# Weaving the xbc projection into the S5 and RG-LRU mixers, and giving the last attention head's norms a step of their own

## The chip, the cores and the metric

One core of one Trainium2 chip runs the whole kernel. The metric is the device time of one execution in microseconds (us), as the median of three runs. The engines are TensorE (PE, with its weight load PEld), VectorE (DVE), ScalarE (ACT), GpSimd (POOL) and SyncE (SP), whose queue issues nearly all transfers.

## The reference

Input x is 1024 frames of 1024 features, in two residual blocks. Block 1 is a modulated layer norm, a retention and gated-linear-attention mixer, an output projection and an MLP. Block 2, in which the change lies, is this:

```
proj = x @ w_in                       # split into z, xbc, dt, s5 input, rg input, rg gate
xbc  = silu(causal_conv4(proj_xbc))   # 1024 features, feeds the SSD mixer
s5   : complex diagonal scan h_n = A h_{n-1} + V u, y = readout(h) + local part, gelu, GLU
rg   : x = causal_conv4(proj_rgx); r, g = gates(x)
       h_n = a_n h_{n-1} + sqrt(1 - a_n^2) * g * x, with a from r;  out = h * gelu(proj_gate)
y    = concat(ssd, s5, rg) @ w_out,  residual and layer norm -> h1
attn : 4 heads of 256, over a given memory (softmax(q K^T) V Wo, summed over heads), residual, layer norm -> h2
mlp  : squared-relu MLP on h2, residual, layer norm
```

## The kernel before

All large products are fp32 by three products of rounded halves: `mm3` (L114 to L116) issues high x high, high x low and low x high, each 128x512. A split into halves is a cast on ACT (L82) and a subtraction on DVE (L83); weights come through a staging page S (L91). Features stand on the partitions, two halves h of 512 frames make the columns, so a projection to 128 features takes 2 x 24 = 48 products, 24 into each of two PSUM buffers.

SBUF pages of 128x1024 come from pools (X 8, H 8, W 8, U 4, S 6, bc 3 buffers). Each engine runs its instructions in order. That order is made by a scheduler from dependences and from the order of the code: earlier code goes first where it is ready by the scheduler's own costs, later code fills in where it is not.

`build` runs, in block 2: `dt_proj`, `s5_mixer`, `xbc_proj`, `rg_mixer`, then the SSD blocks woven with the output projection, attention, MLP. The three in the middle are written one after another.

- `s5_mixer`: input transposes, the V products (L1584), a DVE chain of scans and a complex multiplication (L1591 to L1598, `cmul` L1360 to L1365) that gives H; loads of the kernel matrix K in 16 parts (L1609) and of P in two (L1614); the readout, 16 groups of one product with K (L1625) and two with P and H (L1628) for each half m, 48 in all; an addition on DVE (L1638), transposes (L1644), gelu, GLU (L1661 to L1667).
- `xbc_proj`: eight tiles j of 128 features, weights for two at a time. Per half, ACT copies the product (L1193) and makes the last tap (L1194); DVE adds three taps (L1176); ACT takes tanh (L1197); DVE closes the silu (L1198); SP writes it out (L1199).
- `rg_mixer`: projection and convolution; gate weights Wg; plain fp32 gate products (L1329, L1332) with Sigmoid and Tanh; Ln, Exp, Exp and Sqrt on ACT (L1338 to L1343, with the scan L1345 on DVE); then the products of Wg (two tiles, 96 products) whose results are read at L1351 and L1352.
- `attention`: eight parts (4 heads x 2 halves h) in `pipe`, which at each step advances every live part, the oldest first. A part has three steps: scores and softmax; transposes of the probabilities (L1727) and the V products; the Wo products (L1753), added to the residual `acc`. For the last head, hd == 3, the third step also norms each finished tile (`normalize`, L155 to L171), stores it and transposes it (`to_T`: L182 on PE, L186 and the split L82 and L83) for the MLP, whose results ACT reads at L767.

PSUM tiles are all named ps here; `order` rows give them numbers.

Of the kernel before, what the change touches and what calls it, by code (L numbers as in the profile page):

```python
# [14 lines left out]
S = 1024  # L15
# [1046 lines left out]
class Mix2(Mix1):  # L1062
# [116 lines left out]
    def xbc_proj(self, T):  # L1179
        nc, I = self.nc, self.I  # L1180
        hw = self.small([128, 40], tag="hw", bufs=1)
        nc.vector.tensor_scalar(out=hw[:, 0:32], in0=self.pvec("ssd_conv_w"), scalar1=0.5, scalar2=None, op0=ALU.mult)
        nc.vector.tensor_scalar(out=hw[:, 32:40], in0=self.pvec("ssd_conv_b"), scalar1=0.5, scalar2=None, op0=ALU.mult)
        self.s_xd = self.dram([128, 8, S], "s_xbc")
        for c in range(4):
            W = self.wcols(I["w_in_2"], 512 + 256 * c, 256)
            for m in range(2):
                j = 2 * c + m
                raw, o = self.page("X"), self.page("X")
                for h in range(2):  # L1190
                    sl = slice(512 * h, 512 * h + 512)
                    ps = self.feat_out(T, W, slice(128 * m, 128 * m + 128), h)
                    nc.scalar.copy(out=raw[:, sl], in_=ps)  # L1193
                    nc.scalar.activation(out=o[:, sl], in_=ps, func=ACTF.Identity, scale=hw[:, 4 * j + 3:4 * j + 4],  # L1194
                                         bias=hw[:, 32 + j:33 + j])
                self.conv(o, raw, hw[:, 4 * j:4 * j + 4])
                nc.scalar.activation(out=raw, in_=o, func=ACTF.Tanh)  # L1197
                nc.vector.scalar_tensor_tensor(out=o, in0=raw, scalar=1.0, in1=o, op0=ALU.add, op1=ALU.mult)  # L1198
                nc.sync.dma_start(out=self.s_xd[:, j, :], in_=o)  # L1199

    def ssd_setup(self):
        self.s_St = self.half()
# [88 lines left out]
    def rg_mixer(self, T):  # L1291
# [19 lines left out]
        for m in range(2):  # L1311
            raw, xc = self.page("X"), self.page("X")
            for h in range(2):
                sl = slice(512 * h, 512 * h + 512)
                ps = self.feat_out(T, Wx, slice(128 * m, 128 * m + 128), h)
                nc.scalar.copy(out=raw[:, sl], in_=ps)
                nc.scalar.activation(out=xc[:, sl], in_=ps, func=ACTF.Identity, scale=cw[:, 4 * m + 3:4 * m + 4],
                                     bias=cb[:, m:m + 1])
            self.conv(xc, raw, cw[:, 4 * m:4 * m + 4])
            xcs.append(xc)  # L1320
        Wg = self.wcols(w, 2056, 256)
        ms = []
        for m in range(2):
            xc = xcs[m]
            r, gx, t = self.page("H"), self.page("H"), self.page("H")
            for h in range(2):
                sl = slice(512 * h, 512 * h + 512)
                ps = self.ps("tr")
                nc.tensor.matmul(out=ps, lhsT=gw[:, 0, m], rhs=xc[:, sl], start=True, stop=True)  # L1329
                nc.scalar.activation(out=r[:, sl], in_=ps, func=ACTF.Sigmoid, bias=ba[:, m:m + 1])  # L1330
                ps = self.ps("tr")
                nc.tensor.matmul(out=ps, lhsT=gw[:, 1, m], rhs=xc[:, sl], start=True, stop=True)  # L1332
                nc.scalar.activation(out=gx[:, sl], in_=ps, func=ACTF.Tanh, scale=0.5, bias=sm[:, 6 + m:7 + m])
            nc.scalar.activation(out=t, in_=r, func=ACTF.Tanh, scale=sm[:, 2 + m:3 + m])
            nc.vector.scalar_tensor_tensor(out=gx, in0=gx, scalar=1.0, in1=xc, op0=ALU.add, op1=ALU.mult)
            ms.append((xc, r, gx, t))
        for m, (xc, r, gx, t) in enumerate(ms):
            nc.scalar.activation(out=xc, in_=t, func=ACTF.Ln, bias=1.0)  # L1338
            nc.scalar.activation(out=xc, in_=xc, func=ACTF.Exp, scale=-1.0)
            nc.scalar.activation(out=r, in_=r, func=ACTF.Exp, scale=sm[:, m:m + 1])  # L1340
            nc.vector.tensor_tensor(out=t, in0=t, in1=xc, op=ALU.mult)
        for m, (xc, r, gx, t) in enumerate(ms):
            nc.scalar.activation(out=t, in_=t, func=ACTF.Sqrt, scale=0.5)  # L1343
            nc.vector.tensor_tensor(out=gx, in0=gx, in1=t, op=ALU.mult)
            nc.vector.tensor_tensor_scan(out=t, data0=r, data1=gx, initial=0.0, op0=ALU.mult, op1=ALU.add)  # L1345
        for m, (xc, r, gx, t) in enumerate(ms):
            x, q = self.page("X"), self.page("X")
            for h in range(2):
                sl = slice(512 * h, 512 * h + 512)
                ps = self.feat_out(T, Wg, slice(128 * m, 128 * m + 128), h)  # L1350
                nc.scalar.activation(out=x[:, sl], in_=ps, func=ACTF.Copy, scale=0.5)  # L1351
                nc.scalar.activation(out=q[:, sl], in_=ps, func=ACTF.Square)  # L1352
            self.gelu(x, q, q)
            nc.vector.tensor_tensor(out=t, in0=t, in1=q, op=ALU.mult)
            nc.sync.dma_start(out=self.rg_od[:, m, :], in_=t)
# [192 lines left out]
    def s5_mixer(self, T):  # L1548
# [19 lines left out]
        for m in range(2):  # L1568
            for q in range(2):
                ps = self.ps("tr")  # L1570
                for j in range(4):
                    g = 4 * q + j
# [17 lines left out]
        Are, Aim, t = page(), page(), self.page("H")  # L1590
# [12 lines left out]
        a = [v3(x)[:, :, i0] for x in (Are, Aim)]  # L1603
        p = [v3(x)[:, :, i0] for x in (co, sn)]
        self.cmul(v3(H[0])[:, :, i1], v3(H[1])[:, :, i1], a, p, v3(t)[:, :, i1])
        M = [self.page("H") for _ in range(2)]
        for m in range(2):
            for s in range(8):
# [9 lines left out]
        for m in range(2):  # L1618
            ps = self.ps("sc").rearrange("p (r a c) -> p r a c", r=2, c=128)
            for j in range(4):  # L1620
                a = 4 * m + j
                for r in range(2):
                    rs = slice(64 * r, 64 * r + 64)
                    g = 2 * a + r
# [22 lines left out]
                nc.scalar.activation(out=q[:, sl], in_=ps, func=ACTF.Square)  # L1647
            self.gelu(x, q, x)
            Y.append(x)
        gw = self.half([128, 2, 256])  # L1650
        nc.sync.dma_start(out=gw, in_=I["s5_glu_w_2"].rearrange("(k p) e -> p k e", p=128))
        gb = self.small([128, 8], tag="s5t", bufs=20)
# [2 lines left out]
        for m in range(2):  # L1655
            g, o = self.page("H"), self.page("H")
# [25 lines left out]
    def attn_part(self, T, hd, h, st8):  # L1682
# [55 lines left out]
        for t4 in range(4):  # L1738
            t = 4 * h + t4
# [8 lines left out]
            for n in range(2):  # L1748
# [1 line left out]
                ps = self.ps("sc")[:, 0:512]  # L1750
                self.mm3(ps, [(oh[:, m, ts], ol[:, m, ts]) for m in range(2)], [(a[:, 0, c], b[:, 0, c]) for a, b in Wo])
                self.add_res(acc[t][:, c], ps, hd == 0)
            if hd == 3:  # L1753
                if t == 0:
                    st8["T"] = self.new_T()
                self.normalize(acc[t], acc[t], True)
                nc.sync.dma_start(out=_rows(self.h2d, t), in_=acc[t])
                self.to_T(acc[t], t, st8["T"], self.pvec("ln2_g_2"), self.pvec("ln2_b_2"))
# [24 lines left out]
def build(tc, I, out):  # L1783
    from contextlib import ExitStack
    with ExitStack() as ctx:
        n = Mix2(tc, ctx, I, out)
        n.modulation()
        n.kv_mem()
        def run(g):
            while True:  # L1790
                try:
                    next(g)
                except StopIteration as e:
                    return e.value
# [7 lines left out]
        T, steps = None, [3, 0, 1, 0, 1]  # L1802
        while T is None:
# [4 lines left out]
            T = next(norm)  # L1808
# [11 lines left out]
        T = run(n.block1_out())  # L1820
        T = n.block1_mlp(T)
        n.dt_proj(T)
        n.s5_mixer(T)
        n.xbc_proj(T)
        n.rg_mixer(T)
        n.ssd_setup()
        n.wout = n.wout_load(I["w_out_2"])
        out = n.block2_out()
# [90 lines left out]
```

## Time and profile before

| what | value |
|---|---|
| median of three runs | 2733.69 us (2730.89 to 2739.81) |
| the profiled execution, its own time | 2723.2 us |
| its span | 2721.4 us |
| mean granted TensorE clock | 0.964 |
| PE busy | 2572.5 us (95%) |
| DVE busy | 1908.2 us (70%) |
| ACT busy | 1113.8 us (41%) |

PE is busy nearly throughout, and a busy matmul record says nothing of the clock it ran at: a granted clock of 1.00 is the higher level (2.4 GHz), 0.50 the lower (1.2 GHz). The tables by stretch give both side by side, the timeline gives the distance from one instruction to the next. Some matmul records are missing from the trace, and one plain fp32 product shows as two records.

### The profile page before, as it was taken

How to read it: one execution, taken by the hardware profiler on the slowest of the kernel's cores; microseconds unless marked ns; L12 is line 12 of the kernel's file. 1: busy time of each engine (PE TensorE's matmuls, PEld its weight loads, DVE VectorE, ACT ScalarE, POOL GpSimd, SP SyncE). 2: the span in 40 equal slices, each digit the busy share in tenths (PEclk: the TensorE clock that was granted, in tenths of full speed). 3: DMA queues.
4: the chain of work that ended last, by engine and by line, in shares of the span. 5: the costliest groups of instructions: out<-in, count | busy, mean ns of one | idle time of the engine just before them, and what ended most of it. 6: DMA issues, size and time to landing. Idle time of an engine off the chain costs nothing.

```text
span 2721.4 us, 32892 instructions
## 1 busy us (share of the span) xinstructions
PE 2572.5 (95%) x12086; PEld 2085.6 (77%) x12086; DVE 1908.2 (70%) x3237; ACT 1113.8 (41%) x1669; POOL 265.8 (10%) x238
## 2 busy tenths in 40 slices
PE   7898999889999999999999997999997999999997
PEld 7576777677888888888876765778876888888885
DVE  5847765788897777555954558785566877767759
ACT  3522233224654444433642462452236444444332
POOL 4112135540000000000000004200000000000000
PEclk8899999999999999999997998999998999999998
DMA  9674423454266669857641313371101756699774
GB/s 332 210 232 142 147 98 102 142 150 147 78 224 217 214 234 324 287 177 240 202 153 47 110 62 105 111 242 40 54 21 73 246 195 224 230 325 333 271 234 145
DMA packets 255130, 484.36 MB, mean 178 GB/s; under 512 B 21604, under 2 KB 110964, under 8 KB 254968
## 3 DMA queue, kind: packets, MB, share of 16 engines
q1 hardware_dynamic: 247768, 470.59, 51.3%
q10 hardware_dynamic: 7200, 11.67, 1.2%
q8 instruction: 95, 1.56, 0.2%
q14 instruction: 67, 0.55, 0.1%
HBM read 338.80 MB, written 143.38 MB: 177 GB/s over the span
## 4 chain that ended last, share of the span: by engine, by line
PE 76%; DVE 10%; DMA 4%; ACT 4%; issue 3%; POOL 2%; SPq 0%; ACTq 0%; DVEq 0%; POOLq 0%
PE ps L114 23%; PE ps L116 23%; PE ps L115 23%; ACT half L186 1%; PE ps L182 1%; DMA H<-r_qk 1%; DVE half L543 1%; POOL X L522 1%; DMA H<-g_qkb 1%; DMA bc<-in_w_ada 1%; DVE st L155 1%; PE ps L1628 1%; DVE W L83 1%; PE ps L535 1%; POOL W L83 0%
## 5 line engine op out<-in xcount | busy, mean ns | idle before, releaser
L114 PE MATMUL ps<-U,W 128*128 128x512 f32 (+1 forms) x1080 | 426.2, 395 | 11.4 <-ACT X L1352 5.9
L83 DVE TENSOR_TENSOR W<-S,W 128x1024 fp32r<-128x1024 f32 (+1 forms) x272 | 332.8, 1225 | 147.9 <-ACT W L82 145.9
L114 PE MATMUL ps<-W,H 128*128 128x512 f32 x1088 | 425.1, 391 | 3.6 <-DVE sm L167 3.0
L115 PE MATMUL ps<-U,W 128*128 128x512 f32 (+1 forms) x1080 | 424.1, 393 | 0.1
L115 PE MATMUL ps<-W,H 128*128 128x512 f32 x1088 | 424.0, 390 | 0.0
L116 PE MATMUL ps<-W,H 128*128 128x512 f32 x1088 | 423.9, 390 | 0.0
L116 PE MATMUL ps<-U,W 128*128 128x512 f32 (+1 forms) x1080 | 423.5, 392 | 0.0
L82 ACT CAST W<-S 128x1024 fp32r<-128x1024 f32 x288 | 299.2, 1043 | 282.0 <-PE ps L115 200.0
L83 DVE TENSOR_TENSOR H<-S,H 128x1024 fp32r<-128x1024 f32 x130 | 158.8, 1222 | 149.3 <-ACT H L82 138.5
L82 ACT CAST H<-S 128x1024 fp32r<-128x1024 f32 x130 | 136.5, 1050 | 288.6 <-PE ps L115 211.9
L114 PEld LDWEIGHTS ps<-U,W 128*128 128x128 f32 (+1 forms) x1080 | 201.1, 186 | 59.9 <-ACT X L1352 6.3
L114 PEld LDWEIGHTS ps<-W,H 128*128 128x128 f32 x1088 | 204.6, 188 | 47.7 <-DVE X L1014 3.7
L115 PEld LDWEIGHTS ps<-U,W 128*128 128x128 f32 (+1 forms) x1080 | 201.1, 186 | 47.0 <-DVE U L336 2.5
L116 PEld LDWEIGHTS ps<-W,H 128*128 128x128 f32 x1088 | 204.4, 188 | 42.2 <-DVE H L83 0.2
L115 PEld LDWEIGHTS ps<-W,H 128*128 128x128 f32 x1088 | 204.6, 188 | 41.9
L116 PEld LDWEIGHTS ps<-U,W 128*128 128x128 f32 (+1 forms) x1080 | 200.7, 186 | 45.0 <-issue 0.7
L114 PE MATMUL ps<-W,U 128*128 128x512 f32 x352 | 142.0, 403 | 0.0
L115 PE MATMUL ps<-W,U 128*128 128x512 f32 x352 | 140.6, 399 | 0.2 <-DVE W L83 0.2
L116 PE MATMUL ps<-W,U 128*128 128x512 f32 x352 | 140.4, 399 | 0.1
L767 ACT ACTIVATE ev<-ev 128x512 f32<-128x512 f32 x104 | 65.5, 630 | 138.8 <-DVE ev L865 117.3
L1239 POOL TENSOR_TENSOR half<-tri,s_adt 128x512 f32<-128x512 f32 x16 | 19.6, 1233 | 884.5 <-DVE half L1116 778.2
L768 ACT ACTIVATE X<-ev 128x512 f32<-128x512 f32 x128 | 81.1, 636 | 3.5
(527 smaller groups left out, 4606.5 us busy)
## 6 DMA issues: line engine op xcount, KB each, us to landing
S<-mlp_h SPq DMA_DIRECT2D x112, 512.0 KB, 4.8
S<-in_w_ff SPq DMA_DIRECT2D x96, 512.0 KB, 5.1
mlp_h<-X SPq DMA_DIRECT2D x96, 512.0 KB, 3.9
S<-in_mlp_w SPq DMA_DIRECT2D x96, 512.0 KB, 5.2
mlp_w<-S SPq DMA_DIRECT2D x96, 256.0 KB, 2.8
S<-mlp_w SPq DMA_DIRECT2D x48, 512.0 KB, 4.8
S<-in_w_in SPq DMA_DIRECT2D x46, 512.0 KB, 5.2
bc<-in_w_ada SPq DMA_DIRECT2D x32, 512.0 KB, 5.0
```

Source lines behind the costliest of these rows:

```text
L82: self.nc.scalar.copy(out=hi, in_=src)
L83: (lo_eng or self.nc.vector).tensor_tensor(out=lo, in0=src, in1=hi.bitcast(F32), op=ALU.subtract)
L114: mm(out=ps, lhsT=lh, rhs=rh, start=start and k == 0, stop=False)
L115: mm(out=ps, lhsT=lh, rhs=rl, start=False, stop=False)
L116: mm(out=ps, lhsT=ll, rhs=rh, start=False, stop=stop and k == n - 1)
L155: self.nc.vector.bn_stats(out=st[:, h, :], in_=y[:, h * 512:(h + 1) * 512])
L182: nc.tensor.transpose(ps[:, j * 128:(j + 1) * 128], y[:, k * 128:(k + 1) * 128], self.ident)
L186: nc.scalar.activation(out=full[:, j * 128:(j + 1) * 128], in_=ps[:, j * 128:(j + 1) * 128], func=ACTF.Identity, scale=scale[:, k:k + 1], ...
L522: nc.gpsimd.tensor_tensor(out=E[:, l, :].rearrange("p (g c) -> p g c", c=2 * w), in0=bv, in1=bv[:, :, w - 1:w].broadcast_to([128, 64 // w, ...
L535: nc.tensor.matmul(out=ps[:, r, u, :], lhsT=k[rs] if l < 0 else E[rs, l, :], rhs=q[rs] if l < 0 else qt[rs, l, :], start=True, stop=True)
L767: nc.scalar.activation(out=r, in_=x, func=ACTF.Relu)
L768: nc.scalar.activation(out=out, in_=r, func=ACTF.Square)
```

## The change

`xbc_proj` becomes a generator that yields after each feature tile, and its two pages per tile come from the pools S and bc instead of X. `s5_mixer` yields after H is made and before the GLU; `rg_mixer` yields after the convolutions, after the gates and after the scans. `build` advances the xbc generator at those points: three tiles after s5's first yield and one after its second, one after rg's first and three after its second. In attention the norms, the store and the transposes of the last head leave the Wo loop and become a fourth step of their part, so that `pipe` runs those of h = 0 beside the third step of h = 1.

```diff
@@ xbc_proj
-                raw, o = self.page("X"), self.page("X")
+                raw, o = self.page("S"), self.page("bc")
...
                 nc.sync.dma_start(out=self.s_xd[:, j, :], in_=o)
+                yield
@@ rg_mixer
             xcs.append(xc)
+        yield
         Wg = self.wcols(w, 2056, 256)
...
             ms.append((xc, r, gx, t))
+        yield
         for m, (xc, r, gx, t) in enumerate(ms):
             nc.scalar.activation(out=xc, in_=t, func=ACTF.Ln, bias=1.0)
...
             nc.vector.tensor_tensor_scan(out=t, data0=r, data1=gx, initial=0.0, op0=ALU.mult, op1=ALU.add)
+        yield
         for m, (xc, r, gx, t) in enumerate(ms):
             x, q = self.page("X"), self.page("X")
@@ s5_mixer
         self.cmul(v3(H[0])[:, :, i1], v3(H[1])[:, :, i1], a, p, v3(t)[:, :, i1])
+        yield
         M = [self.page("H") for _ in range(2)]
...
             Y.append(x)
+        yield
         gw = self.half([128, 2, 256])
@@ attn_part
-            if hd == 3:
-                if t == 0:
-                    st8["T"] = self.new_T()
+        if hd == 3:
+            yield
+            if h == 0:
+                st8["T"] = self.new_T()
+            for t in range(4 * h, 4 * h + 4):
                 self.normalize(acc[t], acc[t], True)
                 nc.sync.dma_start(out=_rows(self.h2d, t), in_=acc[t])
                 self.to_T(acc[t], t, st8["T"], self.pvec("ln2_g_2"), self.pvec("ln2_b_2"))
@@ build
-        n.s5_mixer(T)
-        n.xbc_proj(T)
-        n.rg_mixer(T)
+        xbc = n.xbc_proj(T)
+        for g, side in ((n.s5_mixer(T), (3, 1)), (n.rg_mixer(T), (1, 3))):
+            for _ in g:
+                for _ in range(side[0] if side else 0):
+                    next(xbc, None)
+                side = side[1:]
+        run(xbc)
```

Lines behind an inserted yield shift: the readout's L1625 and L1628 become L1630 and L1633, `cmul` L1360 to L1365 become L1364 to L1369, the scans L1598 become L1602, the transposes L1727 become L1733.

On PE, at the readout of s5, this is where xbc's first tile (its second PSUM buffer is ps1984) ends before:

```order
L116 MATMUL ps1984_11966<-U956_6101,W1980_11933 128x512
L1625 MATMUL ps1952_11792<-H1947_11768,X1929_11677 128x128
L1625 MATMUL ps1958_11841<-H1948_11769,X1930_11678 128x128
L1628 MATMUL ps1952_11792<-H1949_11786,X1945_11758 128x128
L1628 MATMUL ps1958_11841<-H1949_11786,X1945_11758 128x128
```

And the same place now; ps1961 belongs to xbc's second tile, ps1970 to its third, ps1977 to the readout:

```order
L116 MATMUL ps1961_11875<-U956_6101,W1953_11780 128x512
L114 MATMUL ps1970_11922<-U954_6099,W1963_11909 128x512
L115 MATMUL ps1970_11922<-U955_6100,W1963_11909 128x512
L1630 MATMUL ps1977_12006<-H1972_11982,X1929_11677 128x128
L116 MATMUL ps1970_11922<-U954_6099,W1964_11910 128x512
```

Before, the whole readout stands behind 48 products of xbc and the other seven tiles behind the readout. Now tiles 0, 1 and 2 and a part of tile 3 stand ahead of the first product with P (L1633, 62 rows further down), and 46 products of the readout stand together inside tile 3.

On DVE, at the end of s5's scans and in its complex multiplication, before:

```order
L1361 TENSOR_TENSOR X1945_11758<-X1942_11747,H1939_11741 128x8x127
L1598 SCALAR_TENSOR_TENSOR X1943_11748<-H1941_11743,X1943_11748 128x1024
L1364 TENSOR_TENSOR X1946_11759<-X1942_11747,H1940_11742 128x8x127
L1360 TENSOR_TENSOR H1944_11749<-X1943_11748,H1940_11742 128x8x127
L1362 TENSOR_TENSOR X1945_11758<-X1945_11758,H1944_11749 128x8x127
L1363 TENSOR_TENSOR H1944_11749<-X1943_11748,H1939_11741 128x8x127
L1365 TENSOR_TENSOR X1946_11759<-X1946_11759,H1944_11749 128x8x127
```

Now, with bc1955 the first tile of xbc, and W1964 the low half of the weights of its third and fourth:

```order
L1368 TENSOR_TENSOR X1946_11759<-X1942_11747,H1940_11742 128x8x127
L1364 TENSOR_TENSOR H1944_11749<-X1943_11748,H1940_11742 128x8x127
L1176 SCALAR_TENSOR_TENSOR bc1955_11785<-S1954_11784,hw1947_11768,bc1955_11785 128x1023
L1366 TENSOR_TENSOR X1945_11758<-X1945_11758,H1944_11749 128x8x127
L1176 SCALAR_TENSOR_TENSOR bc1955_11785<-S1954_11784,hw1947_11768,bc1955_11785 128x1022
L1367 TENSOR_TENSOR H1944_11749<-X1943_11748,H1939_11741 128x8x127
L1176 SCALAR_TENSOR_TENSOR bc1955_11785<-S1954_11784,hw1947_11768,bc1955_11785 128x1021
L1369 TENSOR_TENSOR X1946_11759<-X1946_11759,H1944_11749 128x8x127
L1198 SCALAR_TENSOR_TENSOR bc1955_11785<-S1954_11784,bc1955_11785 128x1024
L83 TENSOR_TENSOR W1964_11910<-S1962_11908,W1963_11909 128x1024
```

The three taps of xbc's first tile stand inside the multiplication that gives H, and the split of the next weights behind the tile's last step. In SP's queue the writes (L1199) of the first two xbc tiles now stand ahead of the two loads of P; before, the loads of P stood ahead of every such write.

On PE, at the end of attention, before; ps2600 to ps2635 are transposes of normed tiles of h = 0, ps2642 is a V product of h = 1:

```order
L182 MATMUL ps2600_15884<-ident_75,X2386_14547 128x128 x4
L182 MATMUL ps2602_15896<-ident_75,X2386_14547 128x128 x4
L1727 MATMUL ps2637_16082<-ident_75,half2584_15819 128x128 x4
L1727 MATMUL ps2637_16082<-ident_75,half2587_15839 128x128 x4
L182 MATMUL ps2611_15942<-ident_75,X2389_14569 128x128 x4
L182 MATMUL ps2613_15954<-ident_75,X2389_14569 128x128 x4
L182 MATMUL ps2622_16000<-ident_75,X2392_14591 128x128 x4
L182 MATMUL ps2624_16012<-ident_75,X2392_14591 128x128 x4
L182 MATMUL ps2633_16058<-ident_75,X2395_14613 128x128 x4
L182 MATMUL ps2635_16070<-ident_75,X2395_14613 128x128 x4
L114 MATMUL ps2642_16097<-H2638_16091,bc2546_15541 128x512
```

Now, behind all 12 V products of h = 1; ps2644 and ps2645 are its first Wo products, ps2613 to ps2622 transposes of h = 0:

```order
L114 MATMUL ps2645_16123<-W2567_15706,H2600_15923 128x512
L182 MATMUL ps2613_15965<-ident_75,X2386_14547 128x128 x4
L116 MATMUL ps2644_16115<-W2567_15706,H2601_15924 128x512
L115 MATMUL ps2645_16123<-W2568_15707,H2600_15923 128x512
L114 MATMUL ps2644_16115<-W2570_15712,H2600_15923 128x512
L115 MATMUL ps2644_16115<-W2571_15713,H2600_15923 128x512
L116 MATMUL ps2645_16123<-W2567_15706,H2601_15924 128x512
L114 MATMUL ps2645_16123<-W2570_15712,H2600_15923 128x512
L182 MATMUL ps2615_15977<-ident_75,X2386_14547 128x128 x4
L182 MATMUL ps2622_16007<-ident_75,X2389_14569 128x128 x4
```

Before, the V and Wo products of h = 1 stand behind every transpose of h = 0; now the V products stand ahead of them and the Wo products between them. On ACT the cast of the probabilities of h = 1 stands ahead of the first norm of h = 0 instead of behind the last one but a tile's rest.

## Rows read from the trace of the kernel before

**Rows 1.** The page's head and its line of busy times.

```profile
span 2721.4 us, 32892 instructions
...
PE 2572.5 (95%) x12086; PEld 2085.6 (77%) x12086; DVE 1908.2 (70%) x3237; ACT 1113.8 (41%) x1669; POOL 265.8 (10%) x238
```

**Rows 2.** Stretches: length, PE, PEld, DVE, ACT, POOL busy, clock, DMA, GB/s.

```profile
1440.11:1636.26 196.15, 183.51 (x735) 142.03 (x734) 108.68 (x94) 90.23 (x116) 2.71 (x3) 0.90 0.21 69
...
1450.00:1460.00 10.00, 3.56 (x12) 2.82 (x12) 7.50 (x6) 0.00 (x0) 0.00 (x0) 0.63 0.00 0
1460.00:1470.00 10.00, 10.00 (x34) 7.53 (x33) 0.00 (x0) 0.00 (x0) 0.00 (x0) 0.50 0.00 0
...
1490.00:1500.00 10.00, 10.00 (x29) 5.33 (x29) 7.75 (x7) 7.79 (x13) 0.00 (x0) 0.99 0.00 0
...
1530.00:1540.00 10.00, 10.00 (x46) 8.29 (x45) 7.25 (x6) 4.53 (x6) 0.00 (x0) 1.00 0.39 129
...
1620.00:1630.00 10.00, 6.11 (x21) 4.93 (x22) 8.61 (x8) 7.44 (x11) 0.00 (x0) 0.83 0.17 51
```

**Rows 3.** What PE waited for, 1390 to 1640 us: total, times, longest.

```profile
PE ps L114 <- ACT X L1352: 5.9, 1, 5.9
PE ps L1628 <- DVE X L1362: 5.4, 1, 5.4
PE ps L1628 <- DVE X L1365: 1.3, 1, 1.3
```

**Rows 4.** Timeline of PE: start, length, line, operation, count.

```profile
1458.38 0.79 PE L1625 MATMUL ps<-H,X 128*128 128x128 f32 x2
...
1475.24 1.97 PE L1644 MATMUL ps<-ident,H 128*128 128x128 f32 x8
...
1503.85 0.39 PE L115 MATMUL ps<-U,W 128*128 128x512 f32 x1
...
1507.25 0.39 PE L115 MATMUL ps<-U,W 128*128 128x512 f32 x1
...
1596.79 1.02 PE L1329 MATMUL ps<-X,H 128*128 128x512 f32 x2
1597.64 1.02 PE L1332 MATMUL ps<-X,H 128*128 128x512 f32 x2
```

**Rows 5.** Timeline of DVE: s5's last multiplication, one xbc tile.

```profile
1456.39 1.22 DVE L1365 TENSOR_TENSOR X<-X,H 128x1016 f32<-128x1016 f32 x1
...
1511.97 3.92 DVE L1176 SCALAR_TENSOR_TENSOR X<-X,hw,X 128x1023 f32<-128x1023 f32 x3
1517.08 1.23 DVE L1198 SCALAR_TENSOR_TENSOR X<-X,X 128x1024 f32<-128x1024 f32 x1 [1.19 <-ACT X L1197]
```

**Rows 6.** Timeline of ACT: a table load among rg's gates.

```profile
1598.99 1.28 ACT L1330 ACT_TABLE_LOAD   x1
```

**Rows 7.** DMA issues of 1400 to 1640 us: KB each, median us to landing.

```profile
H<-s_P SPq DMA_DIRECT2D x2, 512.0 KB, 4.5
```

**Rows 8.** Stretch of the SSD's start, columns as in Rows 2.

```profile
1640.00:1650.00 10.00, 5.71 (x18) 3.13 (x16) 10.00 (x8) 2.62 (x4) 9.92 (x7) 0.69 0.14 41
```

**Rows 9.** Stretches at attention's end, columns as in Rows 2.

```profile
2032.95:2090.64 57.69, 40.34 (x185) 31.40 (x183) 36.14 (x101) 43.82 (x94) 0.00 (x0) 0.83 0.18 73
...
2040.00:2050.00 10.00, 4.12 (x18) 2.93 (x17) 2.86 (x6) 10.00 (x23) 0.00 (x0) 0.50 0.25 105
...
2070.00:2080.00 10.00, 10.00 (x53) 8.20 (x52) 7.84 (x27) 9.63 (x22) 0.00 (x0) 1.00 0.27 107
```

**Rows 10.** Timeline of ACT at attention's end.

```profile
2068.60 1.05 ACT L82 CAST W<-S 128x1024 fp32r<-128x1024 f32 x1 [10.11 <-PE ps L115]
2069.55 1.24 ACT L171 ACTIVATE X<-X,sm,sm 128x1024 f32<-128x1024 f32 x1
...
2090.64 1.27 ACT L767 ACTIVATE ev<-ps 128x512 f32<-128x512 f32 x2
```

**Rows 11.** A stretch of one-column products (L228, L230), columns as in Rows 2.

```profile
72.00:74.00 2.00, 2.00 (x19) 2.00 (x18) 0.00 (x0) 0.00 (x0) 0.00 (x0) 0.92 0.95 322
```

## The prediction

> **What bounds the kernel now.** I read the page first: PE is busy 95% of 2721.4 us, DVE 70%, ACT 41% [rows 1]. So an edit pays only where PE waits, or is busy at the lower clock. The tables by stretch find such places, and the change touches two of them. In the first, from the end of s5's V products to the first product behind Wg, 196.15 us, the mean clock is 0.90; a good stretch next to it has PE 10.00 of 10 at 1.00 [rows 2]. At 1450 PE is busy 3.56 of 10 while DVE works, and the clock falls; at 1460 PE is busy 10.00, but at 0.50, and 1490 is the first stretch near 1.00 again [rows 2]. The waits say what PE lacked: 5.4 and 1.3 us for s5's complex multiplication, and 5.9 us for ACT before Wg's products, in the stretch at 1620 [rows 2, 3]. The second place is attention's end. From the first norm of h = 0 to the MLP's first result, 57.69 us, ACT is busy 43.82, more than PE's 40.34 or DVE's 36.14 [rows 9]; its longest idle, 10.11 us, ends just before the first norm of h = 1, and the MLP's L767 stands behind the last of these norms [rows 10]. ACT's in-order chain, and PE's work for h = 1 between its two parts, set that end.
>
> **First term, the stretch of 196.15 us.** Nothing is removed but waits; so I add up PE's work as the new order has it. 15 products stand between 1503.85 and 1507.25, which makes 0.2267 us each at full clock [rows 4]. In the stretch fall 384 products of xbc less the 6 that stand before it, and 192 of rg: 570 x 0.2267 = 129.2. The readout repeats a group from 1458.38 to 1475.24 nine times, 1.873 each, so 16 groups are 30.0 us at half clock [rows 4]. Its price at full clock is not in the trace: a clock twice as fast gives 15.0 at the least overhead, none of the time scaling gives 30.0. I take 15.0, since the order puts 512-column products up to the first P product and behind the last, and PE no longer idles ahead of it; the other end is a rival. Two times eight transposes, 1.97 at half clock, are some 2.0 together at full. A plain fp32 product costs 1597.64 - 1596.79 = 0.85 [rows 4]: eight in the GLU, eight gates, and two score products of the SSD that the order still has inside, 15.3. Together 161.5.
>
> Then the waits that the weave brings. The three taps of an xbc tile take 3.92 on DVE, its closing step 1.23 behind a wait of 1.19 for tanh [rows 5]. They enter s5's multiplication, which ended at 1456.39 + 1.22 = 1457.6 [rows 5]; with three taps in it, less what overlaps, it ends near 1461.5. PE has 96 products ahead instead of 48 and comes there only near 1440.1 + (96 - 6) x 0.2267 = 1460.5, and the rest of tile 2 and part of tile 3 still stand ahead of the first product with P. So the 5.4 and 1.3 go. What is late next is the low weights of tiles 2 and 3: their split stands behind tile 0's last step, at about 1461.5 + 1.2 + 1.2 = 1464, while PE wants it at 1460.5 + 4.4, the cost of 96 products having ended at 1462: about 2. The same pattern stands before the GLU (1.7 by the same step of 1.2 behind a tap) and before tiles 6 and 7 (2.7: a table load of 1.28 [rows 6] and a tap). ACT has nine table loads from the gates on where it had seven, and the chain Ln, Exp, Sqrt now has tiles 5 to 7 beside it instead of nothing; so the 5.9 goes, and I put 3.2 for two PSUM buffers of Wg that ACT empties behind a tanh. The sum of new waits is 9.6. Its ends are 0, if buffers hide all, and 21, four times the 5.15 of taps and closing step [rows 5].
>
> 161.5 + 9.6 = 171.1, so 25.0 less than 196.15. Not all is kept: before, SSD block 0 had begun inside this stretch, in the idle time of PE; now its front comes behind Wg. There POOL is busy 9.92 of 10 and DVE 10.00 [rows 8], so its start can't be squeezed. Between 0 (all beside Wg) and 5.9 (all of what it filled) I take 3.0. **The term is -22.0.**
>
> The other edits of this part cost nothing by this: the pages in S and bc hold a tile until its tanh is read or its write has landed, and writes of tiles three apart are over 30 us apart, against transfers that land within 5 [rows 7]. One is less safe. The loads of P stood ahead of all xbc writes in SP's queue and now stand behind those of tiles 0 and 1; they are issued when tile 1 is closed, near 1462 + 1.4 + 6.3 (its convolution, from 1511.97 to 1518.31 [rows 5]) + 1 = 1471, and land 4.5 later [rows 7], at 1475.5. PE reaches the first P product after 96 + 48 + 15 products, at 1440.1 + 153 x 0.2267 + 2.0 = 1476.8. The slack is about 1 us; the loads of K and weights beside them stay ahead.
>
> **Second term, attention's end.** The V and Wo products of h = 1 (12 and 48) no longer wait for ACT to finish h = 0; PE works on them while ACT norms h = 0, and the statistics for h = 1 are there when ACT comes to them. From the chain of 57.69 goes its idle time, 57.69 - 43.82 = 13.9, less about 0.8 that PSUM and the first transposes keep: 13.1. It starts later, since the transposes of the probabilities and their cast (about 1 us each) and the last statistics now precede the first norm: 3.8. So -9.3, with ends of -5 (the start slips as far again) and -13.1. DVE has 57.69 - 36.14 = 21.6 us to spare for the splits [rows 9].
>
> **The sum.** -22.0 - 9.3 = -31.3. The profiled execution took 2723.2, its span 2721.4; the median of the runs is 2733.69, 10.5 above. The terms are differences, so a profiled span would be near 2690 and the median 2733.69 - 31.3 = **2702.4**. The ends of the terms (-11.4 and +9.6 of waits, +-3 of the SSD, +-4 of attention) hardly meet: 2692 to 2715 is this case's own range.
>
> **Rival A: the readout falls to half clock all the same.** 46 of its products still stand in a row without a 512-column product. For it: in a run of one-column products PE was recorded busy 2.00 of 2 us and the clock still went to 0.92 on its way down [rows 11], so busy records alone don't hold it, and 31 us of the readout at 0.50 did not raise it before 1490 [rows 2]. Against it: 128 columns are not one, the transposes among products at 2070 kept 1.00 [rows 9], and at full clock the row is half as long. P's loads landing late would start the same fall, from a slack below 1 us. Price: 30.0 - 15.0, up to 2717, with part of the row at full clock 2710. Chance 0.16.
>
> **Rival B, the slower side: the convolution's round trip paces PE.** The mechanism is ACT's one queue from the gates to Wg: the copy that empties PSUM stands behind the previous tile's tanh, that behind the taps on DVE, and rg's table loads between them. If each tile ran in series, PE would stand for 6.3 us per tile [rows 5], over six tiles of xbc and two of Wg 50 us. It becomes slower than before when more than 31.3 + 9.6 = 41 of the 50 come true, between six and seven tiles of eight, and would give 2702.4 - 9.6 + 50 = 2743. Against it: before, the same round trip ran beside PE at 10.00 of 10, DVE 7.25 and ACT 4.53 [rows 2]. Chance 0.05.
>
> **Rival C: attention keeps its time.** If the clock drops while h = 0's transposes stand between the Wo products, the 60 products take twice 0.2267, 27.2 us, and 32 transposes some 8; started at 2037 they end at 2072, and the statistics of h = 1 come no sooner than the 2069.55 of before [rows 10]. Then 2702.4 + 9.3 = 2712. For it speaks the stretch at 2040, mere transposes with waits, at 0.50; against it that at 2070, transposes among products, at 1.00 [rows 9]. The Trainium skill, "TensorE: Matmul & The Clock Gate", section "Part 4: PE-mode transpose", says that transposes don't count as busy for the clock in the same way; by it this rival would be the likely one, and the stretch at 2070 of this trace decides for me against it. Chance 0.11.
>
> **Rival D: the weave moves the waits only.** New waits at their end of 21 and the SSD's front at 5.9 leave 25.0 - 11.4 - 5.9 = 8 of the first term; with attention in full 2716, with neither in full about 2727. Chance 0.06.
>
> **How the numbers follow.** My case has 0.62 and gives 2702. A, C and the better half of D lie between 2710 and 2717, so 2690 to 2722 holds 8 in 10 with a margin for a sum of two of them. What a measurement can tell from no change is 0.3%, 8.2 us, 2725.5: only B, D's worse half, and A with C together and a little more lie behind it. Faster 0.87, same 0.08, slower 0.05.
>
> **What would show it.** In the profile after: no wait of 5 us before the readout, and the stretch of the readout at 1.00 and about 15 us long (at 0.50 it is A); no wait of PE on L1355 or L1356 near Wg; waits of PE on ACT's L1193 and L1194 of some 3 us in all (many times 6 is B); from the start of tile 0 to the end of Wg 171 us. At attention's end an ACT busy almost without idle, and its last norms some 9 us sooner against the end of Wo's products for h = 0. The forecast is wrong if either stretch keeps its length.

## The result, and the profile after

The changed kernel takes 2689.64 us (median of four runs, 2687.85 to 2690.42) beside 2732.29 us of the kernel before (2730.53 to 2739.81): a ratio of 0.9838, 95% interval 0.9818 to 0.9857, or 42.7 us less. The forecast was 2702 with a range of 2690 to 2722; the result lies 0.4 us below its lower end, and the gain is 11 us larger than the 31.3 forecast. Two later comparisons with fresh runs of both kernels gave 0.9860 (0.9837 to 0.9883) and 0.9866 (0.9843 to 0.9889). Their medians were 2688.32 beside 2722.13 and 2686.29 beside 2723.05, so 34 and 37 us less. The changed kernel took nearly the same in all three comparisons; it is the kernel before that took some 10 us more in the first.

The two profiles stand closer to the forecast than the medians do: the spans are 2721.4 [rows 1] and 2688.5, 32.9 us apart. Where these go is read by comparing when the same point of the program is reached in both profiles: the V products end 1.0 later in the profile after, the first product behind Wg comes 25.8 earlier (1610.50 for 1636.26), attention's first scores 25.4 earlier, the MLP's first result 34.0 earlier (2056.61 for 2090.64), the end 32.9 earlier.

The first stretch after, from the product behind V to the first behind Wg, and slices of it; columns as in Rows 2. It answers to [rows 2]:

```profile
1441.08:1610.50 169.42, 166.12 (x720) 127.25 (x719) 108.30 (x93) 92.66 (x117) 2.45 (x2) 1.00 0.30 98
1450.00:1460.00 10.00, 10.00 (x46) 8.29 (x45) 10.00 (x9) 2.53 (x4) 0.00 (x0) 1.00 0.00 0
1460.00:1470.00 10.00, 8.52 (x37) 6.50 (x37) 8.95 (x8) 4.96 (x6) 0.00 (x0) 1.00 0.29 85
1480.00:1490.00 10.00, 10.00 (x59) 7.48 (x58) 2.76 (x4) 1.06 (x1) 0.00 (x0) 1.00 0.68 218
```

196.15 us became 169.42, the clock 0.90 became 1.00, and PE is busy 166.12 of it. The hole at 1450 is filled, while DVE is busier there than before (10.00 for 7.50), since the taps of xbc now stand inside its multiplication. The larger part of the readout runs in the slice at 1480, at full clock. What PE waits for in this stretch after, which answers to [rows 3]:

```profile
PE ps L114 <- ACT W L82: 2.1, 2, 1.1
PE ps L116 <- DVE W L83: 0.8, 2, 0.5
PE ps L114 <- ACT X L1356: 0.2, 1, 0.2
```

Three waits of 12.6 us in all became five of 3.1: the splits of late weights, as forecast, but shorter; the PSUM buffers of Wg cost 0.2. Two groups of the readout in the timeline of PE, which answer to [rows 4]:

```profile
1480.76 0.49 PE L1630 MATMUL ps<-H,X 128*128 128x128 f32 x2
1481.18 0.71 PE L1633 MATMUL ps<-H,X 64*128 64x128 f32 x4
1481.82 0.49 PE L1630 MATMUL ps<-H,X 128*128 128x128 f32 x2
```

A group takes 1.06 us where it took 1.87 before, so some 16.9 for all sixteen. Attention's end, from the first norm of h = 0 to the MLP's first result, beside the slice in which h = 1 is transposed; it answers to [rows 9]:

```profile
2011.58:2056.61 45.03, 35.99 (x170) 28.25 (x169) 31.96 (x94) 43.06 (x93) 0.00 (x0) 0.92 0.23 94
...
2040.00:2050.00 10.00, 10.00 (x54) 8.09 (x53) 2.77 (x4) 9.84 (x23) 0.00 (x0) 1.00 0.26 104
```

ACT is busy 43.06 of 45.03 us: the idle 13.9 of before shrank to 2.0. At the SSD's start a wait has grown. The row of PE's waits before, from 1600 to 1800, and the three largest after:

```profile
PE ps L1243 <- POOL half L1239: 2.2, 1, 2.2
...
PE ps L182 <- ACT H L171: 5.1, 2, 2.6
PE ps L1244 <- POOL half L1240: 4.8, 1, 4.8
PE ps L1252 <- DVE half L1262: 2.1, 1, 2.1
```

PE waited 2.2 us for POOL's products of the first block (L1239, now L1240); now it waits 4.8 us, since it comes to them sooner.

### The profile page after: what moved, and what is told of

It reads as the page before. It is cut to its first block, busy times and chain, and to the rows that moved or that the text cites. A ratio compares the mean times of both kernels' runs of the same rounds, so it can differ in the third digit from the quotient of the medians.

```text
span 2688.5 us, 32853 instructions
## 1 busy us (share of the span) xinstructions
PE 2560.3 (95%) x12086; PEld 2076.7 (77%) x12086; DVE 1902.7 (71%) x3237; ACT 1114.8 (41%) x1671; POOL 264.1 (10%) x238
## 4 chain that ended last, share of the span: by engine, by line
PE 76%; DVE 9%; issue 4%; DMA 4%; ACT 4%; POOL 3%; SPq 0%; POOLq 0%; ACTq 0%; DVEq 0%
PE ps L114 23%; PE ps L116 23%; PE ps L115 23%; PE ps L182 1%; POOL X L522 1%; DMA H<-r_qk 1%; DMA H<-g_qkb 1%; DMA bc<-in_w_ada 1%; ACT half L186 1%; DVE W L83 1%; DVE half L543 1%; PE ps L535 1%; POOL W L83 0%; DVE bc L1176 0%; DVE st L155 0%
## 5 line engine op out<-in xcount | busy, mean ns | idle before, releaser
L114 PE MATMUL ps<-U,W 128*128 128x512 f32 (+1 forms) x1080 | 426.9, 396 | 10.8 <-ACT ev L767 5.1
L1240 POOL TENSOR_TENSOR half<-tri,s_adt 128x512 f32<-128x512 f32 x16 | 20.1, 1264 | 889.6 <-DVE half L1118 777.9
```

Of the source, the lines that this page charges most:

```text
L114: mm(out=ps, lhsT=lh, rhs=rh, start=start and k == 0, stop=False)
```

## The experiments

**The two parts alone.** Each beside 23 fresh runs of before on the same chip (median 2720.6). The first is the changed kernel with `attn_part` as before; the second is the kernel before with the attention part of the change alone.

```diff
 weave alone, against the changed kernel
-        if hd == 3:
-            yield
...
-            for t in range(4 * h, 4 * h + 4):
+            if hd == 3:
+                if t == 0:
+                    st8["T"] = self.new_T()
 attention alone, against the kernel before
-            if hd == 3:
-                if t == 0:
...
+        if hd == 3:
+            yield
...
+            for t in range(4 * h, 4 * h + 4):
```

> Only the weave of xbc into s5 and rg; attention as before. If the two parts add, this takes 2733 less 26 by the two profiles, and another 0 to 10 less if what the profiled execution of before hides lies in the woven stretch: 2697 to 2707. If the 10 us that the medians gained beyond the profiles lie in attention, it is 2706 to 2708, ratio 0.990; if they lie in the woven stretch 2697, ratio 0.987.

Measured (e1): 2695.18 us, ratio 0.9911 (0.9898 to 0.9924), 25 us less.

> Only the last head's norms as a step of their own. From the two profiles 7 to 9 us less: 2724 to 2726, ratio 0.997, if attention's end holds nothing that the profiled execution hid; 2714 to 2716, ratio 0.9935, if it does.

Measured (e2): 2711.37 us, ratio 0.9974 (0.9961 to 0.9988), 7 to 9 us less. The product of the ratios is 0.9885: 31 us, the sum that was forecast. So neither part holds the 10 us that the first comparison gave beyond the profiles: here the kernel before takes 2720.6 us and not 2732.29. The times of the weave lie within 3.2 us of each other (four runs) and those of attention alone within 15.5 (twelve runs; the 23 of before within 16.1). So the next question was how before's own time varies.

**The kernel before, again.** Five more profiles, the kernel unchanged.

> The kernel before, once more, for a second profile and more times. My reading: the profiled execution shown (2723.2 us) was a lucky one of a kernel whose executions lie between 2723 and 2740, and the part that varies is where the clock falls and rises; then this profile shows another time, nearer 2732, and the stretch from 1440 to 1636 or attention's end is longer in it, by up to 10 us. The rival: the profiled execution is always some 10 us below the others, and this profile again takes 2723 +- 2 with the same two stretches (196 and 57.7 us).

> The kernel before, a third profile. Of the two so far the faster (span 2714.6) has the clock back 10 us earlier inside the readout than the slower (2721.4). If what varies is how long the clock stays low, this profile's span differs from these two as its time at half clock does, 0.45 us for each us at 0.50. The rival: the span varies by something else, and the stages apart from s5 and the SSD's start differ by more than 2 us.

> The kernel before, a fourth profile. If it takes 2728 or more, theory: the surplus over 2724 lies in stages whose clock falls in some executions (the first 640 us, the SSD's start, attention's end), 0.45 us for each us more at 0.50. The rival: the clock's time is the same and the waits are longer (transfers landing later).

> The kernel before, a fifth profile, with the same two theories: time at the lower clock (0.45 us for each us more) or longer waits.

> The kernel before, a sixth profile, with the same two theories: time at the lower clock (0.45 us for each us more) or longer waits.

Measured (e0, e9, e12, e13, e14): profiled executions of 2716.35, 2724.19, 2727.28, 2723.86 and 2732.99 us. The first expectation failed: the second profile is shorter than the first, not longer, so the 2723.2 us of the rows were no lucky execution. With all later runs of before, on four chips, there are 82 executions, from 2712 to 2733 us. Their median is 2722.0 us, so the profile of the rows stands in their middle; five of them reach 2730.5, the shortest of the four runs in the first comparison. Each of the 82 has a mean granted clock: the 18 at 0.960 or less took 2728.6 us (median), the 20 at 0.966 or more 2717.9. So before's time varies with its time at the lower clock.

In us against the profile of the rows, stage by stage. "To V" ends with the V products, the SSD begins with its first transposes (L1219, at 1615.00 in the rows) and ends with attention's first scores:

| profile | time | to V | s5, xbc, rg | SSD | rest |
|---|---|---|---|---|---|
| e0 | 2716.35 | -1.0 | -4.7 | -2.2 | +1.1 |
| e9 | 2724.19 | 0.0 | +0.3 | 0.0 | +0.7 |
| e12 | 2727.28 | -2.3 | 0.0 | +5.3 | +1.1 |
| e13 | 2723.86 | +1.1 | -0.2 | -0.8 | +0.6 |
| e14 | 2732.99 | +2.8 | +0.3 | +5.8 | +0.9 |

The stretch to V, which the change doesn't touch, varies by 5.1 us, s5 with xbc and rg by 5.0, the SSD by 8.0 and the rest by 1.1. In e0, the shortest profiled execution, the stretches of s5 read so (columns as in Rows 2):

```profile
1450.00:1460.00 10.00, 4.61 (x15) 3.42 (x15) 6.45 (x6) 0.00 (x0) 0.00 (x0) 0.64 0.00 0
1460.00:1470.00 10.00, 10.00 (x35) 7.76 (x36) 0.00 (x0) 0.00 (x0) 0.00 (x0) 0.50 0.00 0
1470.00:1480.00 10.00, 10.00 (x46) 7.93 (x45) 3.21 (x4) 2.58 (x5) 0.00 (x0) 0.67 0.00 0
```

The clock falls in the same wait but is back inside the readout, near 1477, where it stayed at 0.50 until 1490 in [rows 2]. The long execution e14 at the SSD's start:

```profile
1650.00:1660.00 10.00, 6.86 (x23) 5.82 (x24) 10.00 (x11) 2.58 (x5) 8.74 (x6) 0.50 0.13 52
1660.00:1670.00 10.00, 8.47 (x23) 5.00 (x22) 6.96 (x12) 1.80 (x4) 2.70 (x2) 0.50 0.09 26
1670.00:1680.00 10.00, 8.89 (x33) 5.87 (x34) 7.03 (x22) 3.38 (x8) 1.86 (x2) 0.60 0.14 31
1680.00:1690.00 10.00, 7.12 (x34) 6.26 (x33) 7.09 (x15) 0.35 (x2) 2.81 (x3) 0.74 0.89 269
```

and the same place in the profile of before that the forecast used, 3 us earlier in time:

```profile
1650.00:1660.00 10.00, 8.40 (x26) 6.62 (x26) 10.00 (x12) 1.32 (x2) 8.41 (x5) 0.50 0.13 52
1660.00:1670.00 10.00, 8.07 (x25) 4.84 (x24) 5.90 (x13) 2.89 (x7) 1.04 (x1) 0.61 0.13 39
1670.00:1680.00 10.00, 5.52 (x28) 3.72 (x29) 9.81 (x28) 2.40 (x6) 3.63 (x3) 1.00 0.63 184
1680.00:1690.00 10.00, 7.49 (x47) 6.03 (x47) 8.94 (x11) 3.67 (x6) 5.92 (x4) 1.00 0.72 207
```

The second has the clock back near 1668; the first gets it back near 1678 and loses it again near 1685. From 1610 to 1770 e14 has 51 us at the lower clock where the rows have 31, and its SSD is 5.8 us longer, 0.28 for each us. The expected 0.45 is not reached in either stage: in s5, e0 has 13.6 us less at the lower clock and is 4.7 shorter, 0.34 for each; and e9 has 13.9 us more in all, 10.3 of them in the stretch to V, and is 1.0 longer. So the theory of these expectations holds in kind, not in its price; that DVE and POOL set the pace for a part of the SSD's start is a likely reason, not shown. The rival, longer waits, falls for e14: in this stage no group of PE's waits differs by over 1 us between the two.

**The changed kernel, again.** Unchanged, in two comparisons.

> The changed kernel, once more, beside more times of before on this chip. If the 10 us that the first comparison gave beyond the two profiles were executions of before that came out long, this ratio is 0.9885 (the product of the two parts' ratios), some 31 us; the rival, that the parts gain more together than apart: 0.984 again.

> The changed kernel against before, a third comparison. If the gain is the sum of the terms, 31 us: ratio 0.9885; if the two further comparisons (0.984 and 0.986) hold, 0.985 to 0.987, 36 to 41 us, since the kernel before also loses, in many executions, what its profiles so far do not show.

Measured: 2688.32 us (e5, four runs), ratio 0.9860 (0.9837 to 0.9883); 2686.29 us (e15, four runs), ratio 0.9866 (0.9843 to 0.9889). The first ratio lies between its two expectations, 0.9885 and 0.984; the second lies within 0.985 to 0.987, as its second expectation said. The three profiles of the changed kernel stand against the profile of before so, with the woven stretch taken to the last reading of Wg's results (L1352, now L1356): the woven stretch -25.4 to -27.0 us, the SSD -0.7 to +0.7, the rest -7.6 in the profile after and -10.8 and -10.5 in the two new ones. At the SSD's start of e15 (Wg ends at 1608):

```profile
1620.00:1630.00 10.00, 7.04 (x19) 4.97 (x20) 8.68 (x11) 1.56 (x3) 7.29 (x6) 0.57 0.35 107
1630.00:1640.00 10.00, 8.47 (x44) 6.05 (x43) 6.77 (x14) 2.53 (x6) 3.34 (x3) 0.92 0.10 26
1640.00:1650.00 10.00, 5.12 (x26) 3.09 (x26) 9.86 (x28) 2.76 (x6) 3.63 (x3) 1.00 0.59 176
```

The clock is low for some 10 us, until 1632. None of the three profiles of the changed kernel has the long low stretch of e12 and e14.

**s5's weave alone, and rg's alone.** Both have attention as before; the edits are against the changed kernel.

```diff
 s5 alone
-for g, side in ((n.s5_mixer(T), (3, 1)), (n.rg_mixer(T), (1, 3))):
+for g, side in ((n.s5_mixer(T), (3, 1)), (xbc, ()), (n.rg_mixer(T), ())):
...
 rg alone
-for g, side in ((n.s5_mixer(T), (3, 1)), (n.rg_mixer(T), (1, 3))):
+for g, side in ((n.s5_mixer(T), ()), (n.rg_mixer(T), (4, 4))):
```

> xbc woven into s5 alone (three tiles and one, the other four after it), rg as before, attention as before. My theory: the waits of 6.7 us and the half clock of the readout go (13 us for the readout, 1 for transposes, some 2 for other products), the 5.9 us before Wg stay: 2711 to 2715 by the profiles. The rival, that most of the gain is rg's gates and the SSD's earlier front: 2722 or more.

Measured (e3): 2705.68 us, ratio 0.9952 (0.9939 to 0.9965), 13 to 15 us less, all five runs between 2705.4 and 2708.4. Its wait for a PSUM buffer of Wg is still there, 5.9 us on L1356. The time lies below the 2711 to 2715 of its theory and far from its rival's 2722. So s5's part gives 13 to 15 us and rg's, on top of it, 10 (2705.68 - 2695.18).

> xbc woven into rg alone, four tiles behind rg's convolutions and four behind its gates; s5 and attention as before. By the difference of the two weaves measured (25 less 15): 10 us less than before, with the spread of before, since the wait before the readout stays. The rival, that rg's part works only behind s5's: 6 us (the wait before Wg alone) or less.

Measured (e6): 2727.87 us, ratio 1.0011 (0.9998 to 1.0024): nothing. PE's waits in it, 1390 to 1660:

```profile
PE ps L1633 <- DVE X L1366: 5.4, 1, 5.4
PE ps L116 <- DVE W L83: 2.9, 1, 2.9
PE ps L1331 <- ACT H L1332: 2.9, 1, 2.9
PE ps L114 <- ACT W L82: 2.6, 1, 2.6
PE ps L1256 <- ACT H L1221: 2.5, 1, 2.5
PE ps L1244 <- POOL half L1240: 2.4, 1, 2.4
PE ps L1334 <- ACT H L1335: 1.4, 1, 1.4
```

The 5.9 us on Wg's evacuation are gone, and 9.8 us of waits for weights and gates stand in their place: with four xbc tiles on either side of the gates, PE comes to the gates before ACT has emptied their buffers, and to late weights. That these meet on ACT is argued from the names in the rows, not tried. With s5 woven, (1, 3), (1, 2) and (2, 2) all gave the 10 us (below). The run doesn't part two readings: that four and four is a bad dealing, and that rg's part works only behind s5's, as the rival said; the dealing (1, 3) without s5's weave was not run.

**A filler in place of the weave.** 30, then 54 products whose result nobody reads, in s5 behind the multiplication; they add work and leave the rest as before.

```diff
+        L, R = self.act_lhs(T, 0), self.act_rhs(T, 0)
+        self.mm3(self.ps("mm"), L + L[:2], R + R[:2])          # long: L + L + L[:2]
```

> The kernel before with 30 products of 128x512 added in s5 whose result nobody reads (6.8 us of work at full clock); no weave. They fill the wait of 5.4 and 1.3 us before the readout. My theory: the readout was slow, and its time varied from one execution to the next, only because PE idled ahead of it and the clock fell; then the readout's group takes 1.06 us instead of 1.87, the kernel is 11 to 16 us faster than before although it does more work, and its times lie within 4 us of each other. The rival: the group of small products needs xbc's products among it, or spreads for another reason; then this takes the time of before, or up to 7 us more, with the spread of before.

Measured (e4): 2716.20 us, ratio 0.9970 (0.9951 to 0.9989), runs from 2704.6 to 2725.9: the expectation fails. The timeline of its PE:

```profile
1457.04 0.48 PE L1630 MATMUL ps<-H,X 64*128 64x128 f32 x2 [0.49 <-DVE X L1365]
1457.46 0.49 PE L1627 MATMUL ps<-H,X 128*128 128x128 f32 x2
1457.88 0.71 PE L1630 MATMUL ps<-H,X 64*128 64x128 f32 x4
1458.51 0.65 PE L1627 MATMUL ps<-H,X 128*128 128x128 f32 x2
1459.09 1.22 PE L1630 MATMUL ps<-H,X 64*128 64x128 f32 x4
```

The long wait is gone, and still the products get longer from 1458.5 on, 1.5 us behind a wait of 0.49 us; they stay so until near 1476. It is the only wait of PE ahead of the readout; the next expectation speaks of two, but the other one, of 0.49 us too, stands at 1482, behind it.

> As the filler before, with 54 unread products instead of 30 (5.4 us more work at full clock), so that PE has no wait at all ahead of the readout. With 30 the clock still fell, some 2 us behind two waits of half a microsecond, and stayed low for 17 us. Theory one: those short waits tipped it; now the readout's group takes 1.06 us throughout, the time is 2706 to 2712 and its spread under 6 us. Theory two: the readout's small products alone let the clock fall when nothing of 512 columns stands among them; then it falls again some 3 us into the readout, the time is 5 us above the short filler's, 2721, and the spread stays at 20 us.

Measured (e8): 2713.39 us, ratio 0.9961 (0.9945 to 0.9978), eight runs within 6.9 us, and the stretches of the readout:

```profile
1450.00:1460.00 10.00, 10.00 (x47) 8.29 (x46) 8.32 (x7) 0.00 (x0) 0.00 (x0) 1.00 0.00 1
1460.00:1470.00 10.00, 10.00 (x57) 7.87 (x55) 0.00 (x0) 0.00 (x0) 0.00 (x0) 1.00 0.01 2
1470.00:1480.00 10.00, 10.00 (x61) 7.58 (x60) 3.81 (x5) 3.12 (x5) 0.00 (x0) 1.00 0.00 0
```

Theory one holds for the clock: with no wait at all ahead of it the readout keeps 1.00 to its end, with no product of 512 columns among its groups, and the spread is 7 us for 21. The time and the spread lie a little above what was expected. The kernel is 11 us faster than before with 54 products (12.2 us) more to do.

Where products of 512 columns stand behind such a wait, the clock came back sooner. In e5 PE waits twice for the late weights of tile 2:

```profile
1462.43 0.50 PE L114 MATMUL ps<-U,W 128*128 128x512 f32 x1 [1.00 <-ACT W L82]
1463.89 0.50 PE L116 MATMUL ps<-U,W 128*128 128x512 f32 x1 [0.47 <-DVE W L83]
1464.71 0.63 PE L116 MATMUL ps<-U,W 128*128 128x512 f32 x1
1468.34 0.39 PE L116 MATMUL ps<-U,W 128*128 128x512 f32 x1
```

The clock falls here too, and the products get longer, 0.63 us for 0.39; but it is back after some 3 us, well ahead of the readout's run of small products.

**Other versions.** w_out's loads behind the first SSD step; and other dealings of the eight tiles.

```diff
 late w_out
-        n.wout = n.wout_load(I["w_out_2"])
...
+        def late(k):
...
+            n.wout = n.wout_load(I["w_out_2"])
...
+        run(n.weave(n.pipe(n.ssd_block(i) for i in range(NB)), late(1)))
 dealings
+  ((n.s5_mixer(T), (3, 2)), (n.rg_mixer(T), (1, 2)))     # more beside s5
+  ((n.s5_mixer(T), (3, 1)), (n.rg_mixer(T), (2, 2)))     # more behind the convolutions
```

> The changed kernel with the loads and splits of w_out moved behind the first step of the SSD blocks. After the change PE waits 4.8 us for POOL at the start of the SSD, where DVE is busy 9 to 10 of 10, a good part of it with these splits. If DVE's splits hold that start back, 4 to 8 us less than the changed kernel; if POOL does (its own chain of products for the first block), within 2 us of it; if the output projection comes late for its weights, up to 5 us more.

Measured (e7): 2700.93 us, ratio 0.9912 (0.9896 to 0.9929), 12.6 above the changed kernel in the same comparison, more than any of the three expectations said. The wait for POOL is 4.2 where it was 4.8, so it is not the splits that hold the SSD's start, and POOL's own chain is what is left. The splits now stand beside the blocks, and PE's waits there have grown, on norms from 5.1 to 10.6 us and on DVE from 2.1 to 7.5:

```profile
PE ps L182 <- ACT H L171: 10.6, 3, 5.5
PE ps L1252 <- DVE half L1262: 7.5, 2, 4.9
PE ps L1244 <- POOL half L1240: 4.2, 1, 4.2
```

> The changed kernel with xbc's tiles dealt 3 and 2 to s5, 1 and 2 to rg (instead of 3, 1, 1, 3). One tile fewer stands behind the gates, so Wg and the SSD's first block come sooner behind the scans. If ACT's chain of Ln, Exp and Sqrt is still covered by two tiles (22 us), the SSD's front gains some of its wait of 4.8 us for POOL: 2 to 5 us less than the changed kernel; if it isn't, a wait before Wg comes back, 2 to 6 us more.

Measured (e10): 2690.62 us, ratio 0.9870 (0.9845 to 0.9896), four runs from 2680.88 to 2695.55.

> The changed kernel with the tiles dealt 3, 1, 2, 2: one tile moved from behind the gates to between rg's convolutions and gates. PE's work is the same; the gates come 11 us later, the chain behind them has two tiles beside it. Within 3 us of the changed kernel if the round trip through ACT doesn't pace PE; 4 us or more above it if the gates' weights or the table loads collide with the extra tile.

Measured (e11): 2688.09 us, ratio 0.9863 (0.9838 to 0.9887). By their ratios both equal the changed kernel. In the first no wait for Wg's buffers came back and the wait for POOL stayed, at 5.1, so neither of its two expectations came; no version beat the changed kernel.

## Why the prediction was right or wrong

- *What bounds the kernel.* Right: both places were those where the time came from. One reading was loose: the 5.9 us on L1352 stand in the middle of Wg's products, not before them; PE waits there for ACT to empty the buffers of the first 48.
- *The readout at full clock.* Right in kind, mis-sized: 16.9 us instead of 15.0 [rows 4], since a group shrinks from 1.87 to 1.06 and not to 0.94. Rival A fell: in none of eight profiles with s5 woven did the clock fall in the readout's run of small products. In three of them (e3, e5, e10) it fell for some 3 us behind the waits for tile 2's weights, and was back some 10 us ahead of that run. The loads of P were issued at 1471.93, as forecast, and PE did not wait for them.
- *The new waits.* Mis-sized: 9.6 forecast, 3.1 measured. The weights of tiles 2 and 3 cost 1.5 where 2 was said, those of tiles 6 and 7 1.4 for 2.7, those before the GLU nothing for 1.7; Wg's buffers cost 0.2 instead of 3.2. No wait stood on L1193 or L1194, where some 3 us were expected. The likely reason, not tried, is that ACT's queue was charged twice, in the stalls and in what the tiles cover. Rivals B and D fell with it.
- *The first stretch as a sum.* 171.1 forecast, 169.42 measured, and that is luck in part: the work came to 166.3 for 161.5, 1.9 of it the readout, while the waits were 6.5 less.
- *The SSD's front.* Mis-sized: 3.0 owed, 0.4 in the profile after and between -0.7 and +0.7 in the three; the wait for POOL grew by 2.6, but the stage lost as much elsewhere. So the first term, from V to attention's first scores, is 26.3 in the profile after (26.1 and 27.6 in e5 and e15), where 22.0 was forecast.
- *Attention.* Right: 9.3 forecast, 8.6 between the profiles (34.0 - 25.4), 7 to 9 alone, and some 11 in the profiles e2, e5 and e15. Its parts came as well: the chain is 12.7 shorter for 13.1, and starts 4.0 later against attention's first scores for 3.8. Rival C fell: the slice at 2040 has transposes among products at 1.00. The Trainium skill ("TensorE: Matmul & The Clock Gate", "Part 4: PE-mode transpose") says that transposes don't count as busy for the clock in the same way. With products among them, at a clock of 1.00, that did not decide here, as [rows 9] had said.
- *The sum.* 31.3 forecast, 32.9 between the two profiles, 36 and 40 between e5, e15 and the profile of before. The step that failed is the last one, "the terms are differences, so ... the median 2733.69 - 31.3". The differences were read in an execution of 2723.2 us and then taken from the median of three runs, 10.5 above it, as if the changed kernel would be 10.5 above as well. Measured: the changed kernel's profiled time, 2690.42, is 0.8 above its median, and its profiled span 2688.5, where the same sentence said near 2690. These 10.5 and 0.8, with the 1.5 by which the profiled times differ more than forecast, make the 12.8 us between 2702.4 and 2689.64. The three runs were the unusual ones, not the profile: 82 later executions of before have a median of 2722.0, and 2722.0 - 31.3 is 2690.7, 1.1 above the result.
- *What stays open.* Why the four runs of the first comparison took 2730.5 to 2739.8 is not known: they have no recorded clock, and no execution of 2740 us was profiled. One way is shown by e12 and e14, which lose 5 to 6 us in the SSD's start, right behind the woven stretch, by a clock that stays low longer; the changed kernel's three profiles don't. Why the clock is low there, from 1610 to 1770, for 24 to 51 us in executions of before and for 14 to 24 in those of the changed kernel was not tried by itself. The two parts alone give 0.9885, the whole 0.984 to 0.987; the intervals of the two later comparisons reach 0.988 and 0.989, so whether the parts gain more together was not settled. The pages from S and bc were part of every woven version and not tried alone.

## What to carry to other kernels

A term that is read in one profiled execution is a difference from that execution. Before it is taken from a median, set the two beside more runs: here three runs lay 10 us above what 82 later ones took, and the profile did not. A wait ahead of a run of small products costs more than itself, since the clock that falls behind it stays low through them, here for 17 to 38 us; independent large products there are worth more than the idle time that they fill, even useless ones. And a dealing has to be tried: the eight tiles put four and four around the gates, with none beside s5, gave nothing.

## What the runs showed of the hardware that was not expected

- One wait of 0.49 us ahead of small products was followed by a granted clock of 0.50 for 17 us while PE was busy throughout; with no wait the same products kept 1.00.
- Waits of 1.00 and 0.47 us among products of 512 columns let the clock fall in three of eight profiles and not in the other five, and where it fell it was back after some 3 us.
- How long the clock stays at 0.50 through the same small products differs between executions of one kernel: back near 1477 in one, from 1488 to 1494 in five others, 4.7 us of the kernel's time.
- The mean granted clock of an execution, recorded without any profile, goes with its time: of 82 executions of before, those at 0.960 or less took 10.7 us more (median) than those at 0.966 or more.
